# Moving the loading and squaring of x to GpSimd, and the scaling of the memory keys, in the opening of a one-core transformer trunk

## The chip, the cores and the metric

The kernel runs on one core of a Trainium2 chip. Its time is the device time of one execution in microseconds; the time of a kernel is the median of several runs. Three runs of the kernel before gave 2388.71 us as their median, from 2387.78 to 2390.03 us. The execution that the profiler recorded took 2389.53 us by itself, of which the span from the first to the last instruction is 2387.8 us; 1.7 us lie around the span.

The engines are named as the profile names them: PE is TensorE's matrix multiply, PEld its weight load, DVE is VectorE, ACT is ScalarE, POOL is GpSimd, SP is SyncE, which here only issues transfers.

## The reference

The computation is one decoder layer on a sequence of 2048 rows of width 1024, with 256 memory rows, all in float32:

```python
mem_n = rmsnorm(mem, mem_norm_g)
h = rmsnorm(x, mix_norm_g)                       # retention and pooling heads
x = x + concat([y_ret, y_pool]) @ w_out
k, v = split(mem_n @ wkv)                        # cross-attention
s = (rmsnorm(x, xa_norm_g) @ wq) . k             # per head
x = x + softmax(s) . v @ wo
x = x + conv_glu_ffn(rmsnorm(x, ffn_norm_g))
return rmsnorm(x, final_norm_g)
```

What matters here is `mem_n`, `k`, `v`, and the sum of squares of each row of `x` that the first `rmsnorm(x, ...)` needs.

## The kernel before

Every float32 product is made of three matmuls. `split` writes the upper half of a tile (rounded to the matmul's type) with ACT and the lower half (the tile less its upper half) with DVE; `passes` (lines 273 to 279) multiplies upper by upper, upper by lower and lower by upper into one PSUM bank. In the profile the three matmuls have lines 276, 277 and 278; ACT's upper halves have line 264 (267 where a gain is multiplied in), and all of DVE's two-input operations have the helper's line 248, or 256 for the form with a scalar.

The kernel opens with `folded_weights`, a generator that prepares weights in which the memory is folded in. Its steps are named in one table by a letter and a number:

- K0 to K7 project the normalised memory to keys. Each takes one 128x1024 tile of `wkv` and 24 matmuls of 256 columns; two steps share a PSUM bank, so four banks hold the keys.
- V0 to V7 do the same for the values. After each second one its bank is split into `vp4`.
- M0 to M3 fold the keys of one head into the score weights: two row tiles of `wqT` (through `row_pair`) and 48 matmuls of 256 columns, evacuated by ACT (line 564).
- O0 to O3 fold the values into the output weights (evacuated at line 583), W0 to W3 the pooling weights (line 611). Their matmuls have 512 columns.

The keys' banks wait for the memory's norm: after K7, `spread` brings the norm as a row to all partitions through two matmuls (line 382) and ACT (line 387), `scaled_keys` multiplies the four banks by it on DVE, and `parted` splits each into `kp4`, from which the score folds read.

The raw tiles come through SP's queue into nine places of 128x1024 (`raws`: three in `R`, two in `S`, four in `Z`), taken in a ring; a transfer into a place waits until the lower half of the tile that lay there is written. The pairs of halves go into five places (`wides`: in `Q`, the two `E`, and two in `G`), also in a ring: the new pair waits until the matmuls that read the old one are done.

Beside the steps, `load_x_wide` loads the eight 128x1024 tiles of `x`, each behind one of the steps 5, 7, 8, 9, 11, 13, 16 and 18 (counted along the table from 0): a transfer on SP's queue (line 652) into one of the nine places, the split into `X`, a square on ACT (line 654) and an addition on DVE to the first tile. Behind step 21 `rows_norm` takes the row norms from the sum through eight small matmuls (line 357).

The tile framework orders each engine's instructions at build time by its own estimate; what is marked by `keep_in_program_order` keeps its place in the order of the marked ones, and `issue_after` puts an instruction behind another one. At run time each engine takes its instructions strictly in that order. GpSimd issues transfers of its own queue only later (lines 1051 and 1054, behind small copies of `halo` at lines 1070 and 1071 that pace them) and computes nothing else in the opening.

## Time and profile before

| | |
|---|---|
| median of three runs | 2388.71 us |
| the profiled execution | 2389.53 us |
| its span | 2387.8 us |
| PE busy | 2368.7 us, 11136 matmuls |
| DVE busy | 1796.6 us |
| ACT busy | 1385.8 us |
| POOL busy | 337.9 us |
| granted TensorE clock, mean over the span | 0.997 |

The busy time of PE is the sum of its matmuls' spans, overlaps taken out; what is missing to the span is time in which PE had nothing to run. A view of waits says for each engine how long it sat idle and which instruction ended that; the timeline lists instructions with their start and duration and gives the idle time ahead of one in brackets, with its releaser.

### The profile page before, as it was taken

Reading aid. Unit: us, or ns where it says so; the run is one execution under the profiler, and the core shown is the slowest. Engines: PE = TensorE matmul, PEld = TensorE weight load, DVE = VectorE, ACT = ScalarE, POOL = GpSimd, SP = SyncE. Lnnn points to the kernel's source line nnn. Section 1 sums busy time; section 2 is a strip of 40 time slices with the busy share of each in tenths; the row PEclk is TensorE's granted clock in tenths of the full one; section 3 lists DMA queues with packets and bytes.
Section 4 is the critical chain, followed back from the end, with each engine's and each line's share of the span. In section 5 each row is a group of like instructions: output and inputs, shape, how many; then the busy total and the mean of one; then the engine's idle time right before and its main releaser. Section 6 shows DMA issues by size and latency. Waiting matters only on the chain.

```text
span 2387.8 us, 33436 instructions
## 1 busy us (share of the span) xinstructions
PE 2368.7 (99%) x11136; PEld 1980.8 (83%) x11136; DVE 1796.6 (75%) x2977; ACT 1385.8 (58%) x2507; POOL 337.9 (14%) x524
## 2 busy tenths in 40 slices
PE   8999999999999999999999999999999999999998
PEld 8888888888888888888888888888888888888886
DVE  8687876885767677866788776977677698877876
ACT  7845554663545545545655555855555577676663
POOL 0056554453041000000000010110000000000000
PEclk9999999999999999999999999999999999999999
DMA  8999999999594235486577564765455489768951
GB/s 308 343 285 294 280 264 285 284 308 310 164 260 123 79 119 159 151 281 228 170 238 251 179 199 135 243 207 176 150 177 188 136 261 316 234 183 284 343 174 73
DMA packets 269453, 527.78 MB, mean 221 GB/s; under 512 B 30048, under 2 KB 50912, under 8 KB 269280
## 3 DMA queue, kind: packets, MB, share of 16 engines
q1 hardware_dynamic: 212176, 402.83, 51.5%
q0 software_dynamic: 40960, 94.40, 16.5%
q10 hardware_dynamic: 16144, 28.43, 3.2%
q8 instruction: 87, 1.43, 0.2%
q14 instruction: 86, 0.70, 0.1%
HBM read 423.30 MB, written 196.61 MB: 260 GB/s over the span
## 4 chain that ended last, share of the span: by engine, by line
PE 97%; DMA 1%; DVE 1%; ACT 0%; issue 0%; SPq 0%; DVEq 0%; ACTq 0%
PE mm L276 30%; PE mm L278 30%; PE mm L277 30%; PE aux L276 1%; PE aux L278 1%; PE aux L277 1%; PE aux L800 1%; PE aux L774 1%; PE aux L785 1%; PE aux L947 1%; PE aux L802 1%; PE aux L357 0%; DMA S<-w_v 0%; DVE Z L248 0%; DMA Xd<-E 0%; PE aux L776 0%
## 5 line engine op out<-in xcount | busy, mean ns | idle before, releaser
L276 PE MATMUL mm<-G,Q 128*128 128x512 f32 (+1 forms) x1445 | 558.4, 388 | 4.3 <-DVE G L248 2.6
L277 PE MATMUL mm<-G,Q 128*128 128x512 f32 (+1 forms) x1445 | 558.7, 387 | 0.2 <-DVE G L256 0.2
L278 PE MATMUL mm<-G,Q 128*128 128x512 f32 (+1 forms) x1445 | 555.8, 387 | 0.2 <-DVE Q L248 0.2
L277 PE MATMUL mm<-G,E 128*128 128x512 f32 (+1 forms) x1072 | 409.4, 382 | 0.0
L276 PE MATMUL mm<-G,E 128*128 128x512 f32 (+1 forms) x1072 | 408.3, 382 | 0.3 <-DVE Z L248 0.3
L278 PE MATMUL mm<-G,E 128*128 128x512 f32 (+1 forms) x1072 | 408.0, 382 | 0.2 <-DVE E L248 0.2
L276 PEld LDWEIGHTS mm<-G,Q 128*128 128x128 f32 x1445 | 271.4, 188 | 60.2 <-issue 2.7
L277 PEld LDWEIGHTS mm<-G,Q 128*128 128x128 f32 x1445 | 271.5, 188 | 54.4 <-DVE G L248 0.4
L278 PEld LDWEIGHTS mm<-G,Q 128*128 128x128 f32 x1445 | 271.5, 188 | 54.4 <-DVE Q L248 0.4
L256 DVE SCALAR_TENSOR_TENSOR Z<-Z,vecs,Z 128x1024 f32<-128x1024 f32 x176 | 224.6, 1280 | 50.6 <-ACT Z L1219 47.0
L248 DVE TENSOR_TENSOR Z<-Z,mm 128x512 f32<-128x512 f32 (+1 forms) x290 | 193.5, 672 | 90.8 <-PE mm L278 88.8
L278 PEld LDWEIGHTS mm<-G,E 128*128 128x128 f32 x1072 | 201.5, 188 | 39.7 <-DVE E L248 0.6
L276 PEld LDWEIGHTS mm<-G,E 128*128 128x128 f32 x1072 | 201.4, 188 | 39.7 <-DVE Z L248 0.8
L277 PEld LDWEIGHTS mm<-G,E 128*128 128x128 f32 x1072 | 201.5, 188 | 38.9
L248 DVE TENSOR_TENSOR Q<-R,Q 128x512 fp32r<-128x512 f32 (+2 forms) x205 | 139.9, 683 | 84.3 <-ACT Q L1156 48.0
L248 DVE TENSOR_TENSOR T<-T 128x512 f32<-128x512 f32 (+4 forms) x196 | 133.9, 689 | 27.2 <-ACT T L424 13.3
L1156 ACT ACTIVATE Q<-R 128x512 fp32r<-128x512 f32 (+1 forms) x123 | 75.7, 617 | 133.0 <-PE mm L277 126.3
L1156 ACT ACTIVATE E<-R 128x512 fp32r<-128x512 f32 (+1 forms) x163 | 100.3, 615 | 71.0 <-PE mm L277 56.7
L1219 ACT ACTIVATE Z<-Z,vecs 128x1024 f32<-128x1024 f32 x88 | 109.1, 1241 | 32.3 <-DVE Z L248 31.3
L1103 ACT ACTIVATE G<-T 128x512 fp32r<-128x512 f32 x180 | 108.3, 623 | 32.4 <-DMA T<-Gd 22.4
L1156 ACT ACTIVATE Q<-S 128x512 fp32r<-128x512 f32 (+1 forms) x81 | 49.9, 616 | 98.6 <-PE mm L277 95.7
L248 DVE TENSOR_TENSOR Q<-S,Q 128x512 fp32r<-128x512 f32 (+1 forms) x112 | 75.9, 678 | 38.8 <-ACT Q L1156 30.1
(425 smaller groups left out, 4430.8 us busy)
## 6 DMA issues: line engine op xcount, KB each, us to landing
T<-Gd SPq DMA_DIRECT2D x168, 256.0 KB, 4.3
Ud<-w_up POOLq DMA_DIRECT2D x132, 256.0 KB, 9.7
Gd<-Z SPq DMA_DIRECT2D x110, 256.0 KB, 2.6
R<-Ud SPq DMA_DIRECT2D x104, 256.0 KB, 2.7
R<-w_up SPq DMA_DIRECT2D x82, 256.0 KB, 2.9
S<-Ud SPq DMA_DIRECT2D x72, 256.0 KB, 2.8
Gd<-T SPq DMA_DIRECT2D x56, 256.0 KB, 3.3
T<-Xd SPq DMA_DIRECT2D x53, 256.0 KB, 4.1
```

Source lines behind the costliest of these rows:

```text
L248: return eng.tensor_tensor(out=out, in0=a, in1=b, op=op)
L256: return dve.scalar_tensor_tensor(out=out, in0=a, scalar=s, in1=b, op0=op0, op1=op1)
L276: pe.matmul(ps, lh, rh, start=start, stop=False, skip_group_check=more)
L277: pe.matmul(ps, lh, rl, start=False, stop=False, skip_group_check=more)
L278: latest[0] = pe.matmul(ps, ll, rh, start=False, stop=stop, skip_group_check=more)
L774: pe.matmul(col(sc, c), self.ch(k, c), self.ch(q, c), start=True, stop=True)
L785: pe.matmul(col(kv, c), col(self.kn.f, c), self.ch(v, c, h * T), start=True, stop=True)
L800: pe.matmul(col(y, c), col(self.pr.f, c), self.ch(v, c, h * T), start=True, stop=self.cur[c] is None)
L802: pe.matmul(col(y, c), self.ch(q, c), self.cur[c], start=False, stop=True)
L1103: one = act.activation(hi, x, AF.Copy, scale=-1.0 if i == 2 else 1.0)
L1156: act.activation(p2[:, 0, :w], self.raw[i].f[:, :w], AF.Copy)
L1219: act.activation(self.c[g].f, a[:, 2:], AF.Identity, bias=cb[:, f : f + 1], scale=cw[2][:, f : f + 1])
```

## The change

It has two parts.

The tiles of x go another way. Each comes through GpSimd's own queue into a double place of the small temporaries `T`; the first four transfers are paced by a copy on ACT and one on GpSimd (`halo`, columns 41 and 42), the other four follow when a place is free. GpSimd squares each tile in place and adds it to the first. The tiles are fetched behind the steps 8 to 11 and split behind the steps 11, 12, 13, 15, 17, 18, 19 and 20; the row norms follow behind step 22 in place of 21. The nine raw places hold weights alone.

The keys are scaled later. At the end of K7 the tiles of V0 and V1 and both row tiles of M0 are loaded and split ahead of the norm, and each of the four banks is scaled, and its halves written, behind the lower half of M0's second row tile. The multiplication, the halves of the keys, the pairs of V2 and M1 and M0's row pairs are marked to keep their program order. The pooling factors' tile is loaded behind step 5.

```diff
@@ wide_pair, row_pair @@
-        def wide_pair(raw, parts=1):
+        def wide_pair(raw, parts=1, kept=False):
...
-                split(raw[:, i * w : (i + 1) * w], *(r[:, i * w : (i + 1) * w] for r in u))
+                split(raw[:, i * w : (i + 1) * w], *(r[:, i * w : (i + 1) * w] for r in u), kept=kept)
@@ project @@
-            u = u0 if n == 0 else wide_pair(second, 2) if n == 1 else wide_pair(load_tile(wkv[n]))
+            u = u0 if n == 0 else wide_pair(second, 2) if n == 1 else ready.pop(0) if n in (KT, KT + 1) else wide_pair(load_tile(wkv[n]), kept="both" if n == KT + 2 else False)
@@ scaled_keys @@
-            tt(dve, ps3, ps3, both, ALU.mult)
-            parted(kp4, n, ps)
+            tc.keep_in_program_order(tt(dve, ps3, ps3, both, ALU.mult))
+            parted(kp4, n, ps, "both")
@@ keys @@
             if n == KT - 1:
+                for v in (KT, KT + 1):
+                    ready.append(wide_pair(load_tile(wkv[v])))
+                ready.extend(row_pair(wqT[dt * P : (dt + 1) * P, :], "both") for dt in range(2))
+                rows = lowest[0].ins
                 spread(rn, [rm.f[:, :NMEM]], late=True, behind=latest[0].ins)
                 for pair in done:
-                    scaled_keys(*pair)
+                    with tc.issue_after(rows):
+                        scaled_keys(*pair)
@@ score_weights @@
-            dp = [row_pair(wqT[(2 * h + dt) * P : (2 * h + dt + 1) * P, :]) for dt in range(2)]
+            dp = [ready.pop(0) if h == 0 else row_pair(wqT[(2 * h + dt) * P : (2 * h + dt + 1) * P, :], "both" if h == 1 else False) for dt in range(2)]
@@ x @@
-    def load_x_wide(k, total):
-
-        r = total if k == 0 else raws.take()
-        f = r.f
-        tc.keep_in_program_order(sp.dma_start(f, xT[k * P : (k + 1) * P, :T]))
+    def fetch_x_wide(k, gate):
+
+        mark = nullcontext()
+        if gate:
+            here, there = halo[:, 41], halo[:, 42]
+            tc.keep_in_program_order(act.activation(here, phalo[:, 0, :2], AF.Copy))
+            mark = tc.issue_after(pool.tensor_copy(there, here).ins)
+        r = TT.take(2)
+        with mark:
+            tc.keep_in_program_order(pool.dma_start(r.f[:, :T], xT[k * P : (k + 1) * P, :T]))
+        return r
+
+    def load_x_wide(k, r, total):
+
+        f = r.f[:, :T]
         split(f, X[:, 2 * k], X[:, 2 * k + 1], mixg[:, k : k + 1], kept="both")
-        tc.keep_in_program_order(act.activation(f, f, AF.Square))
+        tc.keep_in_program_order(tt(pool, f, f, f, ALU.mult))
         if k:
-            tc.keep_in_program_order(tt(dve, total.f, total.f, f, ALU.add))
+            tc.keep_in_program_order(tt(pool, total.f[:, :T], total.f[:, :T], f, ALU.add))
             r.free()
@@ the steps @@
-    wv, total, x_at = [], raws.take(), (5, 7, 8, 9, 11, 13, 16, 18)
+    wv, x_raws, x_from, x_at = [], [], (8, 9, 10, 11), (11, 12, 13, 15, 17, 18, 19, 20)
...
-        if n == 21:
+        if n == 22:
```

How the instructions move is seen in three places. In the rows below, `Q_79`, `E0_73`, `E1_74` and `G_72` on the left of the arrow are halves of tiles (`G_72` also the halves of keys, values and x), `R_78`, `S4_80`, `S5_81`, `Z2_75` on the right are raw places, `mm...` are PSUM banks, `Z3_76` is the staging of folded weights, `T_77` the temporaries, and the brackets name the semaphores waited for.

The first place is ACT around the first score fold M0. Before, from the upper half of V2's tile (`E1_74`) to the evacuation of M0's first bank (`mm19_492`):

```order
L264 ACTIVATE E1_74<-S5_81 128x1024 [waits DMAHW2_49,Activation_49]
L654 ACTIVATE R_78<-R_78 128x1024 [waits DVE_49]
L264 ACTIVATE G_72<-mm7_146 128x2x256 [waits DVE_49]
L264 ACTIVATE G_72<-mm8_203 128x2x256 [waits DVE_49]
L264 ACTIVATE G_72<-mm13_281 128x2x256 [waits DVE_49]
L264 ACTIVATE G_72<-mm14_340 128x2x256 [waits DVE_49]
L267 ACTIVATE G_72<-Z2_75,vecs_82 128x1024 [waits DMAHW3_49]
L264 ACTIVATE G_72<-mm18_422 128x2x256 [waits PE_49]
L267 ACTIVATE G_72<-Z2_75,vecs_82 128x1024 [waits DMAHW5_49]
L264 ACTIVATE G_72<-R_78 128x1024 [waits DMAHW5_49]
L564 ACTIVATE Z3_76<-mm19_492 128x512 [waits PE_49]
```

In the changed kernel, from the evacuation of M0's third bank (`mm21_509`) on; `Q_79` is V3's tile, `E0_73` a row tile of M2, `E1_74` V2's tile, the first `G_72<-T_77` the first tile of x, and the two rows behind it are M1's row tiles (they differ only in their waits):

```order
L570 ACTIVATE Z3_76<-mm21_509 128x512 [waits PE_49]
L264 ACTIVATE Q_79<-Z2_75 128x1024 [waits DMAHW6_49,PE_49]
L264 ACTIVATE E0_73<-R_78 128x1024 [waits DMAHW7_49,PE_49]
L570 ACTIVATE Z3_76<-mm22_523 128x512 [waits PE_49]
L572 DMA Md_102<-Z3_76 128x2x512 [waits Activation_49]
L665 ACTIVATE halo_96<-phalo_97 128x2 [waits Pool_49]
L264 ACTIVATE E1_74<-Z2_75 128x1024 [waits DMAHW3_49]
L665 ACTIVATE halo_96<-phalo_97 128x2 [waits Pool_49]
L267 ACTIVATE G_72<-T_77,vecs_82 128x1024 [waits DMASW0_49]
L264 ACTIVATE G_72<-Z2_75 128x1024 [waits DMAHW4_49]
L264 ACTIVATE G_72<-Z2_75 128x1024
```

V2's upper half stood ahead of all of M0's evacuations and of the keys' halves; now it stands behind M0's last evacuation and behind two upper halves into `Q` and `E0`, which wait for PE because M0's matmuls read those two places. M1's row tiles stand behind the first tile of x.

The second place is DVE around the scaling of the keys. Before:

```order
L248 TENSOR_TENSOR mm7_146<-mm7_146,T_77 128x512 [waits Activation_49]
L248 TENSOR_TENSOR mm8_203<-mm8_203,T_77 128x512
L248 TENSOR_TENSOR mm13_281<-mm13_281,T_77 128x512
L248 TENSOR_TENSOR mm14_340<-mm14_340,T_77 128x512
L248 TENSOR_TENSOR E0_73<-S4_80,E0_73 128x1024 [waits DMAHW1_49,Activation_49]
L248 TENSOR_TENSOR E1_74<-S5_81,E1_74 128x1024 [waits DMAHW2_49,Activation_49]
L248 TENSOR_TENSOR G_72<-mm7_146,G_72 128x2x256 [waits Activation_49]
```

And in the changed kernel:

```order
L248 TENSOR_TENSOR Q_79<-R_78,Q_79 128x1024 [waits DMAHW0_49,PE_49,Activation_49]
L248 TENSOR_TENSOR E0_73<-R_78,E0_73 128x1024 [waits DMAHW2_49,PE_49,Activation_49]
L248 TENSOR_TENSOR mm7_146<-mm7_146,T_77 128x512
L248 TENSOR_TENSOR G_72<-mm18_423,G_72 128x2x256 [waits Activation_49]
L248 TENSOR_TENSOR G_72<-mm7_146,G_72 128x2x256 [waits Activation_49]
L248 TENSOR_TENSOR mm8_203<-mm8_203,T_77 128x512
L248 TENSOR_TENSOR G_72<-mm8_203,G_72 128x2x256 [waits Activation_49]
```

The four multiplications stood together ahead of M0's second row tile and V2's tile; now M0's two row tiles stand first, and each multiplication is followed by the lower halves of its keys. The lower half of the first two value steps (`mm18_423`) has come between the first multiplication and its keys' lower half.

The third place is ACT at the last tile of x. Before, it stands (from `S4_80`) among the evacuations of O0 and O1 (`mm32_748` is the bank of V4 and V5):

```order
L264 ACTIVATE G_72<-mm32_748 128x2x256 [waits PE_49]
L267 ACTIVATE G_72<-S4_80,vecs_82 128x1024
L264 ACTIVATE E1_74<-R_78 128x1024 [waits DMAHW6_49,DVE_49]
L264 ACTIVATE Q_79<-Z2_75 128x1024 [waits DMAHW2_49,DVE_49]
L583 ACTIVATE Z3_76<-mm41_926,rnm_145 128x4x128 [waits PE_49]
```

In the changed kernel it stands (from `T_77`) behind the bank of V6 and V7 (`mm45_967`) and the first evacuation of W0 (`mm55_1093`):

```order
L264 ACTIVATE G_72<-mm45_967 128x2x256 [waits PE_49]
L621 ACTIVATE Z3_76<-mm55_1093 128x4x128 [waits DMAHW0_49,PE_49]
L267 ACTIVATE G_72<-T_77,vecs_82 128x1024 [waits DMASW7_49]
L621 ACTIVATE Z3_76<-mm56_1098 128x4x128 [waits DMAHW1_49,PE_49]
L264 ACTIVATE Q_79<-R_78 128x1024 [waits DVE_49]
```

The last tile of x has moved behind W0's first matmuls, and the row sums' small matmuls, on PE 39 matmuls of 512 columns behind that first evacuation's bank, wait for GpSimd's last addition.

## The prediction

> **What bounds the kernel now.** I read the page first, then PE's waits in the opening, then the timelines of PE, ACT and DVE around each of those waits, because the change touches nothing behind the opening.

> ```profile
> span 2387.8 us, 33436 instructions
> PE 2368.7 (99%) x11136; PEld 1980.8 (83%) x11136; DVE 1796.6 (75%) x2977; ACT 1385.8 (58%) x2507; POOL 337.9 (14%) x524
> PE 97%; DMA 1%; DVE 1%; ACT 0%; issue 0%; SPq 0%; DVEq 0%; ACTq 0%
> ```

> PE is the bound: 97% of the chain that ended last is matmuls, and 2387.8 less 2368.7 leaves 19.1 us in which PE had nothing to run. The change adds and removes no matmul, so it can only move that idle time, and what the clock loses after it. PE's waits of the first 135 us, in total, times and the longest, hold two that count:

> ```profile
> PE mm L276 <- ACT G L264: 3.0, 2, 2.8
> PE mm L276 <- DVE G L248: 2.6, 1, 2.6
> ```

> PE's timeline (start, duration, and in brackets the idle time ahead with its releaser) shows where they lie and what follows:

> ```profile
> 37.56 0.28 PE L278 MATMUL mm<-G 128*128 128x256 f32 x1
> 40.41 0.35 PE L276 MATMUL mm<-G,Q 128*128 128x256 f32 x1 [2.57 <-DVE G L248]
> ...
> 46.11 0.28 PE L278 MATMUL mm<-G,E 128*128 128x256 f32 x1
> 46.23 0.28 PE L276 MATMUL mm<-G,E 128*128 128x256 f32 x1
> ...
> 56.36 0.39 PE L276 MATMUL mm<-G 128*128 128x256 f32 x1 [2.78 <-ACT G L264]
> ...
> 56.70 0.41 PE L276 MATMUL mm<-G 128*128 128x256 f32 x1
> ...
> 59.91 0.37 PE L277 MATMUL mm<-G 128*128 128x256 f32 x1
> 60.12 0.28 PE L278 MATMUL mm<-G 128*128 128x256 f32 x1
> ```

> The first wait (2.57 us) stands between V1's last matmul and M0's first: the keys' halves are late. M0 then runs into V2 without a gap (46.11 to 46.23, 0.12 us a matmul of 256 columns). The second wait (2.78 us) stands inside M1. Behind it, from 56.70 to 60.12, the matmuls start 0.21 us apart: 16 of them take 3.42 us where 16 times 0.12 is 1.92, so 1.5 us go to a halved clock. The opening thus loses 2.57 + 2.78 + 1.5 = 6.85 us; that is all the change could give back.

> **The change part by part.** The second wait is a transfer's, as the chain of waits shows (start, length):

> ```profile
> 47.34 1.24 DVE R L248
> 48.60 6.63 DMA R<-wqT
> 55.25 1.06 ACT G L264
> ```

> M1's row tile waits for the place in `R` that x's sum of squares held. With x off those places, the changed SP order has M1's tiles right behind V2's, ahead of M0's matmuls: that cause goes, and with it 2.78 us. SP's queue loses eight issues, and nothing else there waited for them. ACT loses eight squares (group of the opening: count, total, mean ns), DVE seven additions of 1.22 us (row 49.62 below), all beside matmuls:

> ```profile
> L654 ACT ACTIVATE Z<-Z 128x1024 f32<-128x1024 f32 x4 | 4.2, 1061 | 0.8 <-DVE G L256 0.8
> ```

> The first wait does not go. These are the durations for it, from the timelines of PE (row sums, then the norm's spread), ACT and DVE, and the landing times of x's transfers on SP's queue:

> ```profile
> 22.97 0.50 PE L357 MATMUL aux<-consts,R 128*128 128x1 f32 x4
> 31.69 0.40 PE L382 MATMUL aux<-Q,ones 128*128 128x256 f32 x2
> 33.58 0.36 ACT L387 ACTIVATE T<-aux 128x256 f32<-128x256 f32 x1
> 36.70 2.03 ACT L264 ACTIVATE G<-mm 128x512 fp32r<-128x512 f32 x4
> 34.91 2.49 DVE L248 TENSOR_TENSOR mm<-mm,T 128x512 f32<-128x512 f32 x4
> 39.58 2.48 DVE L248 TENSOR_TENSOR G<-mm,G 128x512 fp32r<-128x512 f32 x4
> DMA to landing us min/median/max: 5.0/7.9/9.9
> ```

> The spread ends at 32.09, ACT's row at 32.5, M0's two upper halves (0.95 us apart, below) at 34.4, their lower halves at 35.7, the first multiplication (2.49 / 4 = 0.62) at 36.3. That is 1.5 us ahead of V1's end at 37.84, which covers a late row tile: issued behind the row sums at about 23.4, it lands by 23.4 + 9.9 = 33.3 at the worst, 0.8 us late. But in DVE's new order the lower half of V0 and V1 stands between the multiplication and the keys' lower half, and ACT has the same order; that bank is complete only at 37.84. So ACT writes its upper half to 38.5 and the keys' to 39.0 (0.51 each, 0.1 a handover); DVE its lower half to 39.2 and the keys' to 39.8 (0.62 each). M0's first matmul starts at 39.1, its second at 39.95: idle 2.0 us in place of 2.57. Ends: 1.5, and 2.6 if nothing is gained.

> A new wait comes behind M0. For it I need ACT's and DVE's rows of before at the same place, and GpSimd's copy that paces x:

> ```profile
> 46.04 0.58 ACT L564 ACTIVATE Z<-mm 128x512 f32<-128x512 f32 x1
> 46.52 1.05 ACT L264 ACTIVATE Q<-Z 128x1024 fp32r<-128x1024 f32 x1
> 47.46 1.05 ACT L264 ACTIVATE E<-Z 128x1024 fp32r<-128x1024 f32 x1
> 48.41 0.58 ACT L564 ACTIVATE Z<-mm 128x512 f32<-128x512 f32 x1
> 119.33 0.19 ACT L1070 ACTIVATE halo<-consts 128x2 f32<-128x2 f32 x1
> 119.58 0.68 POOL L1071 COPY halo<-halo 128x2 f32<-128x2 f32 x1 [119.13 <-ACT halo L1070]
> 48.49 1.22 DVE L248 TENSOR_TENSOR Q<-Z,Q 128x1024 fp32r<-128x1024 f32 x1
> 49.62 1.22 DVE L248 TENSOR_TENSOR R<-R,Z 128x1024 f32<-128x1024 f32 x1
> ```

> M0's other 47 matmuls run from 39.95 to 45.6. In the new ACT order V2's upper half is queued behind the upper halves into `Q` and `E0`, which wait for M0's last reads, and behind M0's fourth evacuation; the rows of before show those three at 46.52, 47.46 and 48.41, right behind M0's end at 46.23. Nothing is queued there now that PE needs; in the changed kernel PE's next matmul is. ACT gets to it late: the three other banks cost 0.62 + 0.51 + 0.62 and handovers, some 1.9 us each, so the first of them has its upper half at 41.05 and the third at 44.85; the first pacing copy waits for nothing, but the second one, ahead of M0's third evacuation, waits for GpSimd's copy (0.68), until 45.8. Evacuation to 46.3, `Q` to 47.25, `E0` to 48.2, evacuation to 48.7, a pacing copy, V2's upper half to 49.85 and its lower half to 51.1. PE idles from 45.6 to 49.9, runs two matmuls, and idles 0.95 more: 5.25 us. If the pacing cost nothing, `Q` would start at 45.2, 0.4 us ahead of M0's end, and it would be 4.25; with a slower copy, up to 5.9. So the waits are 2.0 + 5.25 = 7.25 in place of 5.35: 1.9 us more.

> The clock's loss I leave at 1.5 us (rows 56.70 to 60.12), at another place: no change. Ends: none, or twice that, since 2.57 us of idle time cost nothing and 2.78 cost 1.5. [...]

> M1's row tiles now stand on ACT and DVE behind the first tile of x, which GpSimd's queue brings. What such a transfer takes is seen later in the trace (timeline of POOL, then the issues, KB each and us to landing):

> ```profile
> 120.19 2.25 POOL L1054 DMA_DIRECT2D Ad<-w_qkgu x4
> 125.72 0.84 POOL L1051 DMA_DIRECT2D Ad<-w_qkgu x1 [2.15 <-DMA Ad<-w_qkgu]
> Ad<-w_qkgu POOLq DMA_DIRECT2D x48, 256.0 KB, 8.4
> ```

> Issued at about 45.7, x lands 5.5 (120.19 to 125.72) to 8.4 us later, at 51.2 to 54.1. Behind it come x's halves and the lower halves of two row tiles, 1.15 + 1.2 + 1.15 + 1.15 = 4.65: 55.9 to 58.8. PE needs the last of these 34 matmuls behind 51.1 (22 of V2, 12 of M1), at 51.1 + 4.1 + 1.5 = 56.7. I take a landing at 52.7: 0.6 us more, ends 0 and 2.1.

> GpSimd's own work is 15 operations of 128x1024 with two inputs, whose kind no row shows. Bounds: the same on DVE takes 1.22 us; of 128x2, GpSimd's copy takes 0.68 us where ACT's takes 0.19, so it is 0.5 longer, or 3.6 times as long: 1.7 to 4.4 us. With two elements a row what differs is a start, not a rate, so I take the lower, 1.7. Its chain starts at x's second tile (squared behind the lower half that ACT and DVE now write last of the first four), about where V4's matmuls begin. From there to the row sums PE has 144 matmuls of 256 columns and 115 of 512. The rate of the wide ones, W's evacuations, and both halves of a tile of x:

> ```profile
> 104.19 0.40 PE L278 MATMUL mm<-Q 128*128 128x512 f32 x1
> 104.42 0.39 PE L277 MATMUL mm<-Q 128*128 128x512 f32 x1
> ...
> 108.17 1.09 ACT L611 ACTIVATE Z<-mm 128x512 f32<-128x512 f32 x2 [0.59 <-PE mm L278]
> 53.77 1.15 ACT L267 ACTIVATE G<-Z,vecs 128x1024 fp32r<-128x1024 f32 x1 [3.21 <-DMA Z<-xT]
> ...
> 43.77 1.27 DVE L256 SCALAR_TENSOR_TENSOR G<-Z,vecs,G 128x1024 fp32r<-128x1024 f32 x1
> ```

> 144 x 0.12 + 115 x 0.23 = 43.7 us for 14 operations and four issues of 0.9: room for 2.85 us an operation. At the end, from W0's first bank to the row sums, PE has 39 x 0.23 = 9.0 us, and against it stand 0.55 (evacuation) + 1.15 and 1.27 (x's halves) + 0.4 (handovers) + two operations: room for 2.8. At 1.7 nothing waits. [...]

> Sum: +1.9 (waits) + 0 (clock) + 0.6 (M1) + 0 (row sums) = +2.5 us. On the profiled execution, 2389.5 us, that gives 2392.0; the median of the runs is 0.8 us below that execution, so I forecast 2391.2. The case's own ends, all of one side at once: -1.1 (4.25, 1.5, no loss of clock, no wait in M1) and +6.8 (5.9, 2.6, twice the loss, 2.1 in M1), so 2387.6 to 2395.5.

> **The rivals.** *GpSimd and DVE hold each other up: slower.* If operations with two inputs in SBUF cannot run on both at once, the time is their sum. Between the lower halves of x's second and last tile stand 12 of GpSimd's operations and, on DVE, 15 such of 128x1024 (1.15 us apart) and 7 of 128x512 (0.62): 20.4 + 21.6 = 42.0 us at 1.7, 55.2 at 2.8 (above which the next rival holds), in the 38.8 us that PE's 34.8 (144 x 0.12 + 76 x 0.23) and the halves around them leave. PE then waits 3.2 to 16.4 us, and 0.5 more for the last two. With the sum: 2395 to 2408, middle 2401.5. It decides from 1.43 us an operation, where the two sums pass 38.8. For it: DVE is busy with two-input work in every stretch here. Against: the trace has no such operation on GpSimd, and its small copies pass beside DVE's. [...]

> *GpSimd alone is too slow: slower.* Over 2.85 us an operation, the row sums wait 14 times the excess: at 3.3, 6.3 us, so 2397.5. For it the bound of 4.4, against it that two elements cannot show a rate.

> *Both waits go: faster.* If V2's halves came in time and the keys' too, 6.85 us less the 0.6 in M1 are won: 2382.5. For it: the first multiplication is done 1.5 us before V1 ends; against it the order of ACT, which is fixed in the program.

> *The change does nothing here.* The stalls only change place and the clock is spared: within the forecast's own range, 2388.7.

> **How the numbers follow.** Forecast 0.47, mutual blocking 0.30, GpSimd too slow 0.14, faster 0.06, no effect 0.03. A measurement of this kernel tells about 0.2% from no change, 4.8 us: bounds 2383.9 and 2393.5. Faster 0.06; slower 0.30 + 0.14 + 0.02 of the forecast's upper end = 0.46; same the remaining 0.48. The range from 2387.6 to 2405 leaves out the faster case and the dearest third of mutual blocking, 0.16 in all; it is wide because blocking has no row.

> **What would show it.** Right: idle of about 2 us ahead of M0 that ends with DVE's lower half; 4 to 6 us behind M0 released by ACT's and DVE's halves into `E`; M1 with little or none; the row sums without a wait for POOL. DVE's 128x1024 rows at 1.22 us between 70 and 110 us, and POOL's at 1.7 to 2.5, speak against blocking; means well above these, with a wait `PE aux <- POOL`, prove it. The forecast is wrong if V2 does not wait, or if PE waits for x's sum.

## The result, and the profile after

The changed kernel takes 2407.56 us (median of 4 runs, 2404.07 to 2412.53) against 2388.65 us before on the same chip: a ratio of 1.008, 95% interval 1.0062 to 1.0099, or 19 us more. The forecast was 2391.2, the range reached to 2405. The profiled execution is the longest of the four, 2412.53 us. Its page, span and engines:

```profile
span 2410.8 us, 33457 instructions
PE 2379.3 (99%) x11136; PEld 1987.9 (82%) x11136; DVE 1810.6 (75%) x2970; ACT 1380.8 (57%) x2503; POOL 395.6 (16%) x551
```

The span is 23.0 us longer. PE runs the same 11136 matmuls, but is busy 10.6 us longer (2379.3 against 2368.7) and idle 12.4 us longer (31.5 against 19.1). The two need different explanations. First the idle time: PE's waits from 30 to 180 us of the span (total, times, longest), which held 5.8 us before and hold 15.7 now.

```profile
PE mm L277 <- ACT E L264: 4.3, 1, 4.3
PE mm L278 <- DVE G L248: 4.0, 2, 3.8
PE mm L278 <- DVE Q L248: 3.0, 1, 3.0
PE aux L358 <- POOL T L248: 2.4, 1, 2.4
PE mm L277 <- DVE G L248: 1.5, 1, 1.5
PE mm L279 <- DVE E L248: 0.5, 1, 0.5
```

The 1.5 is the first wait, ahead of M0; the 4.3 and 0.5 stand behind M0, for V2's halves; M1 has no wait any more. These are as forecast. The 3.0 and 3.8, for lower halves that VectorE writes late, and the 2.4 at the row sums, for GpSimd's last addition, are not. GpSimd's timeline, and VectorE's at the same times (start, duration; a row with x2 gives the sum of two):

```profile
79.94 5.26 POOL L248 TENSOR_TENSOR T<-T 128x1024 f32<-128x1024 f32 x2
86.10 5.29 POOL L248 TENSOR_TENSOR T<-T 128x1024 f32<-128x1024 f32 x2
...
118.85 8.43 POOL L248 TENSOR_TENSOR T<-T 128x1024 f32<-128x1024 f32 x2 [5.90 <-DVE G L256]
```

```profile
79.85 3.09 DVE L248 TENSOR_TENSOR G<-R,G 128x1024 fp32r<-128x1024 f32 x1 [5.04 <-ACT Z L570]
82.87 3.42 DVE L248 TENSOR_TENSOR Q<-Z,Q 128x1024 fp32r<-128x1024 f32 x1
86.21 6.26 DVE L248 TENSOR_TENSOR E<-S,E 128x1024 fp32r<-128x1024 f32 x2
...
118.69 1.21 DVE L248 TENSOR_TENSOR Q<-R,Q 128x1024 fp32r<-128x1024 f32 x1
119.83 1.21 DVE L248 TENSOR_TENSOR G<-S,G 128x1024 fp32r<-128x1024 f32 x1
120.97 1.28 DVE L248 TENSOR_TENSOR E<-Z,E 128x512 fp32r<-128x512 f32 x2
122.39 2.69 DVE L248 TENSOR_TENSOR G<-R,G 128x1024 fp32r<-128x1024 f32 x1
```

VectorE's operation beside one of GpSimd's takes 3.09, 3.42, 3.13 us in place of 1.2, and it ends some 1.1 us behind GpSimd's: the pairs of GpSimd's operations end at 85.20 and 91.39, the operations of VectorE beside them at 86.29 and 92.47. In these rows, then, it stands still until GpSimd's is over and then does its own work. Where VectorE has one operation right behind another (from 118.69), it is GpSimd that waits: 8.43 us for two, where the pairs at 79.94 and 86.10 took 5.3. How full that makes VectorE is seen from the busy time of PE, PEld, DVE, ACT and POOL between 80 and 120 us, before and then after (an operation that stands still counts as busy):

```profile
80.00:120.00 40.00, 39.58 (x215) 33.46 (x214) 27.77 (x45) 32.48 (x50) 0.42 (x1) 1.00 0.99 340
```

```profile
80.00:120.00 40.00, 33.17 (x166) 27.52 (x166) 40.00 (x23) 29.20 (x41) 29.76 (x14) 0.91 0.84 267
```

Before, PE was the full one there (39.58 of 40) and VectorE did 45 instructions in 27.77 us; now VectorE shows no free time at all and has got through 23 of its rows.

The busy time: PE's clock. The column behind POOL's is the granted clock. These windows are 3.41 us long:

```profile
46.64:50.05 3.41, 0.00 (x0) 0.00 (x0) 2.36 (x2) 2.96 (x5) 0.90 (x3) 1.00 0.90 295
50.05:53.47 3.42, 2.81 (x11) 2.52 (x12) 3.29 (x3) 3.12 (x5) 2.40 (x3) 0.50 0.81 255
53.47:56.88 3.41, 3.41 (x18) 3.41 (x17) 3.10 (x2) 1.59 (x2) 2.02 (x1) 0.50 1.04 421
...
104.70:108.10 3.40, 0.76 (x5) 0.33 (x3) 3.40 (x3) 2.03 (x3) 1.58 (x2) 1.00 1.08 396
108.10:111.50 3.40, 2.93 (x6) 1.82 (x6) 3.40 (x3) 2.78 (x5) 3.32 (x2) 0.50 1.00 300
111.50:114.90 3.40, 0.00 (x0) 0.00 (x0) 3.40 (x2) 1.81 (x3) 1.45 (x1) 1.00 0.38 119
114.90:118.30 3.40, 3.07 (x7) 2.48 (x8) 3.40 (x6) 1.56 (x3) 0.00 (x0) 0.50 0.16 16
```

In these rows each window in which PE had little to do (0.00, 0.76 and 0.00 us busy) is followed by one at half clock, though PE is busy for 2.81 to 3.07 us by then; behind the wait for V2 it is two. There is a fourth stretch, 128.56 to 135.38, behind the row sums, and a fifth far behind the opening, 609.83 to 613.24. Half clock in a busy window of 3.41 us costs, by my estimate, half of it, 1.7 us (the matmuls of 512 columns start 0.42 us apart from 610.37 on, 0.23 from 602.87 on). Before, there was one such window up to the last 10 us of the span. Taken over slices of 0.2 us, half clock costs 9.5 us of busy time in the opening and 1.7 at 610, against 1.7 before: 9.5 of PE's 10.6 us. Most of the rest is at the very end, where both kernels fall to half clock: there it costs 1.5 us after (2398.42 to 2401.83) and 0.5 before (from 2377.76). The waits sum up to 9.9 in the opening and 2.3 more between 400 and 660 us: 12.2 of the 12.4.

### The profile page after: what moved, and what is told of

It is laid out like the page before. It is cut to its first block, busy times and chain, and to the rows that moved or that the text cites. A ratio compares the mean times of both kernels' runs of the same rounds, so it can differ in the third digit from the quotient of the medians.

```text
span 2410.8 us, 33457 instructions
## 1 busy us (share of the span) xinstructions
PE 2379.3 (99%) x11136; PEld 1987.9 (82%) x11136; DVE 1810.6 (75%) x2970; ACT 1380.8 (57%) x2503; POOL 395.6 (16%) x551
## 3 DMA queue, kind: packets, MB, share of 16 engines
q8 instruction: 87, 1.43, 0.2%
## 4 chain that ended last, share of the span: by engine, by line
PE 93%; DMA 1%; DVE 1%; POOL 0%; ACT 0%; issue 0%; SPq 0%; DVEq 0%; ACTq 0%
PE mm L277 29%; PE mm L279 29%; PE mm L278 29%; PE aux L277 1%; PE aux L279 1%; PE aux L278 1%; PE aux L822 1%; PE aux L796 1%; PE aux L807 1%; PE aux L969 1%; PE aux L824 1%; PE aux L358 1%; DMA S<-w_v 0%; DVE Z L248 0%; DMA Xd<-E 0%; POOL T L248 0%
## 5 line engine op out<-in xcount | busy, mean ns | idle before, releaser
L278 PE MATMUL mm<-G,Q 128*128 128x512 f32 (+1 forms) x1445 | 560.0, 388 | 4.1 <-DVE G L248 4.0
L277 PE MATMUL mm<-G,Q 128*128 128x512 f32 (+1 forms) x1445 | 559.3, 388 | 3.2 <-DVE G L248 1.5
L277 PE MATMUL mm<-G,E 128*128 128x512 f32 (+1 forms) x1072 | 409.6, 383 | 4.6 <-ACT E L264 4.3
L278 PE MATMUL mm<-G,E 128*128 128x512 f32 (+1 forms) x1072 | 410.5, 383 | 0.0
L278 PEld LDWEIGHTS mm<-G,Q 128*128 128x128 f32 x1445 | 272.1, 188 | 59.1 <-DVE G L248 4.9
L277 PEld LDWEIGHTS mm<-G,Q 128*128 128x128 f32 x1445 | 272.0, 188 | 59.0 <-ACT G L264 1.7
L256 DVE SCALAR_TENSOR_TENSOR Z<-Z,vecs,Z 128x1024 f32<-128x1024 f32 x176 | 224.7, 1280 | 50.1 <-ACT Z L1241 45.6
L248 DVE TENSOR_TENSOR Z<-Z,mm 128x512 f32<-128x512 f32 (+1 forms) x290 | 193.6, 672 | 90.9 <-PE mm L279 88.4
L277 PEld LDWEIGHTS mm<-G,E 128*128 128x128 f32 x1072 | 202.5, 189 | 44.2 <-ACT E L264 4.5
L278 PEld LDWEIGHTS mm<-G,E 128*128 128x128 f32 x1072 | 202.6, 189 | 39.0
L248 DVE TENSOR_TENSOR Q<-R,Q 128x512 fp32r<-128x512 f32 (+2 forms) x209 | 143.9, 689 | 89.2 <-ACT Q L1178 48.9
L248 DVE TENSOR_TENSOR T<-T 128x512 f32<-128x512 f32 (+4 forms) x196 | 134.0, 689 | 27.6 <-ACT T L425 13.5
L1241 ACT ACTIVATE Z<-Z,vecs 128x1024 f32<-128x1024 f32 x88 | 109.2, 1242 | 31.0 <-DVE Z L248 30.1
L1178 ACT ACTIVATE Q<-S 128x512 fp32r<-128x512 f32 (+1 forms) x81 | 49.9, 616 | 98.9 <-PE mm L278 96.3
L248 DVE TENSOR_TENSOR E<-aux,E 128x512 fp32r<-128x512 f32 (+1 forms) x136 | 89.2, 658 | 20.7 <-ACT E L1178 15.6
## 6 DMA issues: line engine op xcount, KB each, us to landing
T<-Gd SPq DMA_DIRECT2D x168, 256.0 KB, 4.4
Ud<-w_up POOLq DMA_DIRECT2D x132, 256.0 KB, 9.6
Gd<-Z SPq DMA_DIRECT2D x110, 256.0 KB, 2.7
R<-Ud SPq DMA_DIRECT2D x104, 256.0 KB, 2.7
R<-w_up SPq DMA_DIRECT2D x82, 256.0 KB, 2.9
S<-Ud SPq DMA_DIRECT2D x72, 256.0 KB, 2.8
Gd<-T SPq DMA_DIRECT2D x56, 256.0 KB, 3.3
T<-Xd SPq DMA_DIRECT2D x53, 256.0 KB, 4.1
```

Source lines behind the costliest of these rows:

```text
L248: return eng.tensor_tensor(out=out, in0=a, in1=b, op=op)
L256: return dve.scalar_tensor_tensor(out=out, in0=a, scalar=s, in1=b, op0=op0, op1=op1)
L277: pe.matmul(ps, lh, rh, start=start, stop=False, skip_group_check=more)
L278: pe.matmul(ps, lh, rl, start=False, stop=False, skip_group_check=more)
L1178: act.activation(p2[:, 0, :w], self.raw[i].f[:, :w], AF.Copy)
L1241: act.activation(self.c[g].f, a[:, 2:], AF.Identity, bias=cb[:, f : f + 1], scale=cw[2][:, f : f + 1])
```

## The experiments

Two theories stood at the start. **Blocking**: GpSimd's squares and additions and VectorE's operations exclude each other, which makes halves and sums late. **Elsewhere**: the transfers by GpSimd's queue (A), the new order of keys and row tiles (B), or GpSimd's own length (C) cost it.

### The parts one by one

*Squares and sums off GpSimd*, all else as in the changed kernel:

```
-        tc.keep_in_program_order(tt(pool, f, f, f, ALU.mult))
+        tc.keep_in_program_order(act.activation(f, f, AF.Square))
-            tc.keep_in_program_order(tt(pool, total.f[:, :T], total.f[:, :T], f, ALU.add))
+            tc.keep_in_program_order(tt(dve, total.f[:, :T], total.f[:, :T], f, ALU.add))
```

> x still comes through GpSimd's queue and the keys are scaled as in the changed kernel, but ScalarE squares x and VectorE adds (15 operations off GpSimd). Theory (GpSimd's two-input operations and VectorE's hold each other up): VectorE's 128x1024 halves are back at 1.2 us, the waits of 3.8 and 3.0 us on VectorE and the 2.4 us on GpSimd go, only the 4.3 us behind M0 and 1.5 ahead of it stay; 2391, between 2389 and 2394. Rival A (the transfers of GpSimd's queue and their descriptors slow VectorE): its rows stay at 2.7 us and more, 2403 to 2408. Rival B (the new order of keys and row tiles costs it): 2403 to 2408 with VectorE's rows at 1.2 us.

Measured: 2400.68 against 2391.51 us, ratio 1.0036 (1.0023 to 1.0049). VectorE's groups from 60 to 128 us (count, total, mean ns), and PE's waits:

```profile
L256 DVE SCALAR_TENSOR_TENSOR G<-T,vecs,G 128x1024 fp32r<-128x1024 f32 x7 | 8.8, 1279 | 2.2 <-ACT G L267 2.2
L248 DVE TENSOR_TENSOR G<-R,G 128x1024 fp32r<-128x1024 f32 x4 | 4.9, 1222 | 3.7 <-ACT Z L570 3.1 <-ACT G L264 0.6
```

```profile
PE mm L277 <- ACT E L264: 4.3, 1, 4.3
PE aux L358 <- DVE T L248: 2.2, 1, 2.2
```

All of VectorE's rows of 128x1024 are back at 1.22 to 1.28 us, with x's transfers still on GpSimd's queue: A is out as the cause of the long rows. The waits of 3.0 and 3.8 are gone. But the ratio is above what was expected: the row sums still wait, now for VectorE (they stand earlier in PE's order in this kernel, ahead of W's evacuations), and two stretches of 6.83 us at half clock stay, which cost 5.65 us.

*Only the squares back on ScalarE*: the first pair of lines of that diff alone.

> Only the eight squares go back to ScalarE, the seven additions stay on GpSimd. Theory (mutual blocking): 7 operations of some 2.8 us block in place of 15, the time they take from VectorE is halved and more, and since part of it fell into VectorE's free time most of the loss goes: 2391 to 2398. Rival C (nothing is blocked, GpSimd's chain of 15 is simply too long for the row sums): 2391 to 2393 with VectorE's halves at 1.2 us throughout, the seven additions fitting easily. Rival A or B: 2403 to 2408.

Measured: ratio 1.0042 (1.0027 to 1.0057). The seven additions take 2.4 us each, the last 3.4; VectorE's group `G<-R,G` has a mean of 1473 ns, in the changed kernel 2607. In VectorE's rows that is between the two kernels, as blocking has it; in time it cannot be told from 1.0036. C is out: seven additions in 40 us leave GpSimd idle for more than half of them.

*Only the key part*, and *only the x part*, the rest as before:

> Only the key part of the change: early row tiles and V0 and V1, keys scaled behind the first fold's rows; x as before, through SyncE's queue into the old places, squared on ScalarE and added on VectorE. Theory (blocking): the key part alone costs no more than the order's stalls, 2389 to 2394. Rival B: most of the 19 us is here, 2400 to 2408.

> Only the x part: x in pairs of temporaries by GpSimd's queue, squared and added on GpSimd; keys, V0, V1 and the row tiles as before. Theory (blocking): the loss is here, less the stall behind M0: 2398 to 2406, with VectorE's halves at 2.7 us and more and a wait for GpSimd's sum. Rival B: 2387 to 2391.

Measured: keys alone 1.0065 (1.005 to 1.008), 2408.0 us, where 2389 to 2394 was expected: a miss, and the time is the one that rival B gave. x alone 1.0059 (1.0042 to 1.0076), 2406.6 us, 0.6 above the range expected. The two alone are 15.5 and 14 us, more than the 19 of both together, so the parts don't simply add up. In keys alone V2 is late again (5.2 and 1.9 us), ScalarE having halves and squares of x between M0's last evacuations and V2's half; that is read from its timeline, not tested.

*The x part with its arithmetic off GpSimd*: the first diff on top of x alone.

> x through GpSimd's queue into pairs of temporaries, squared on ScalarE and added on VectorE; keys, V0, V1 and the row tiles as in the kernel before. Theory (blocking by GpSimd's arithmetic, and a price of 1.7 or 3.4 us of clock behind each stall of over 2 us): against x alone with its arithmetic on GpSimd (ratio 1.0059) all waits on VectorE of 3 us and more go, VectorE's rows are at 1.2 us, the stall for the row tile inside M1 is gone too: ratio 0.998 to 1.002. Rival A (x's transfers by GpSimd's queue, or their later landing, cost the time): ratio 1.003 to 1.006.

Measured: ratio 1.0012 (1.0003 to 1.0021). With x through GpSimd's queue there are now four kernels, keys old or new, arithmetic on GpSimd or not:

| ratio to before | arithmetic on ScalarE and VectorE | on GpSimd | GpSimd's arithmetic |
|---|---|---|---|
| keys as before | 1.0012 | 1.0059 | +0.0047, 11 us |
| keys changed | 1.0036 | 1.0080 | +0.0044, 10.5 us |
| the keys' part | +0.0024, 5.7 us | +0.0021, 5.0 us | |

With x in its new places the parts add up: some 11 us for GpSimd's arithmetic, some 5 for the keys, 3 for x in its new places by the other queue. (With x in its old places the keys' part alone cost 15.5 us, as above. The four were timed on more than one chip, each against before; a difference of two carries some 0.002 either way.)

### Does it take two operands?

In place of the products and sums copies, which read one:

```
-        tc.keep_in_program_order(tt(pool, f, f, f, ALU.mult))
+        tc.keep_in_program_order(pool.tensor_copy(f, f) if k else act.activation(f, f, AF.Square))
-            tc.keep_in_program_order(tt(pool, total.f[:, :T], total.f[:, :T], f, ALU.add))
+            tc.keep_in_program_order(pool.tensor_copy(total.f[:, :T], total.f[:, :T]))
```

> Fourteen of GpSimd's fifteen operations are replaced by a copy of the same 128x1024, which reads one operand (the first square goes to ScalarE; the other squares and the sum are left out). Theory (a pair of two-input operations blocks each other): VectorE's 128x1024 halves return to 1.2 us between 60 and 128 us, the waits of 3.8 and 3.0 us go, ratio 1.003 to 1.005 as with squares and sums off GpSimd. Rival (any read of SBUF by GpSimd blocks VectorE for its length): VectorE's halves stay at 2 us and more, ratio 1.005 to 1.009.

Measured: 1.0118 (1.0095 to 1.0141). The time says nothing here, since the row sums have another place in PE's order in this kernel: they run at 135.6 us. Behind the opening PE waits 8.55 us at 175.24 for an upper half; why that one is late was not followed up. The rows do say something. GpSimd, then VectorE:

```profile
80.30 1.05 POOL L678 COPY T<-T 128x1024 f32<-128x1024 f32 x1
...
81.81 1.05 POOL L676 COPY T<-T 128x1024 f32<-128x1024 f32 x1
82.79 1.05 POOL L678 COPY T<-T 128x1024 f32<-128x1024 f32 x1
```

```profile
80.70 4.22 DVE L248 TENSOR_TENSOR G<-R,G 128x1024 fp32r<-128x1024 f32 x1 [3.73 <-ACT Z L570]
```

VectorE's operation, issued at 80.70, ends at 84.92, 1.08 us behind the last copy (83.84): it stood still for three copies, two of which were issued after it. So here a copy that reads one operand blocked as well, 4.22 us in place of 1.2; that rival was right. A copy is over in 1.05 us, so most of VectorE's rows meet none: 3 of its 26 of 128x1024 between 60 and 128 us take over 1.4 us, and the means stay below the rival's 2 us but for `G<-R,G`.

*GpSimd's operations cut in two*: each `tt(pool, ...)` in a loop over the two halves of 512 columns.

> The changed kernel with each of GpSimd's 15 operations of 128x1024 cut into two of 128x512. Theory (GpSimd and VectorE exclude each other by whole instructions): the same total is excluded, VectorE's waits are no longer 2.6 us but up to 1.4 at a time, so its 128x1024 halves take up to 2.6 us and not 3.4; ratio 1.005 to 1.008. Rival (they share a bandwidth, in proportion, not by instructions): no difference to the changed kernel in VectorE's rows, 1.008.

Measured: 1.0066 (1.0044 to 1.0088), whose interval holds the changed kernel's 1.008. The rows went against the expectation: VectorE's `G<-R,G` has a mean of 2864 ns (2607 in the changed kernel) and `G<-T,vecs,G` 2083 (1423), and its longest operation, at 80.67, takes 5.88 us where at most 2.6 was expected. More of VectorE's operations meet one of GpSimd's (12 of 25 of 128x1024 take over 1.4 us, 8 of 25 in the changed kernel); nothing was won. The rival of a shared bandwidth, by which the rows would not change, does not fit them either.

### The stall behind M0 and the clock

*V2's tile early*, loaded and split ahead of the scaled keys, with GpSimd's arithmetic as changed and with it on ScalarE and VectorE:

```
                 rows = lowest[0].ins
+                ready.append(wide_pair(load_tile(wkv[KT + 2]), kept="both"))
```

> The changed kernel, but V2's tile is loaded and split ahead of the scaled keys like V0's and V1's. Theory (each stall of PE costs its own length and then the clock, halved for whole stretches of 3.4 us behind it; the order behind M0 makes one stall, GpSimd's arithmetic against VectorE the others): the 4.3 us behind M0 and the 6.8 us at half clock go, about 7 us less than the changed kernel's ratio of 1.008, so 1.005. Rival (the clock dips belong to the load of the engines, not to stalls): only the 4.3 us go, ratio 1.006, and half speed stays between 50 and 57 us.

> The same, and x squared on ScalarE and added on VectorE, so that GpSimd only issues x's transfers. Theory: of the 10 us of the kernel with squares and sums off GpSimd, the 4.3 us wait and its 2.2 us of clock go; what stays is the wait for the row sums with its half clock, 5.6 us, and the gain of M1's wait: ratio 0.999 to 1.002. Rival (clock by load): ratio 1.002 to 1.004.

Measured: 1.008 (1.0065 to 1.0095) and 1.0051 (1.0034 to 1.0067); neither is better than the kernel without this edit. In the first the wait for V2 and the half clock behind it are gone, as the theory had it (full clock up to 106.7 us), and the time is lost elsewhere: at 199.68 PE waits 3.83 us for VectorE, which has waited 3.59 us for the transfer of `rope_d` (tables of sines that the kernel computes and stores), and half clock stands from 198.90 to 205.72. In the changed kernel no wait between 180 and 390 us is over 0.5 us. In the second the wait for V2 has gone too, and PE waits in M1 instead:

```profile
58.84 0.58 PE L277 MATMUL mm<-G 128*128 128x256 f32 x1 [6.90 <-ACT G L264]
```

```profile
55.35 1.06 ACT L264 ACTIVATE G<-Z 128x1024 fp32r<-128x1024 f32 x1 [2.44 <-DMA Z<-wo]
```

M1's late halves stand on ScalarE behind a tile of `wo` that waits for its transfer. (The profiled execution of this second kernel, 2394.71 us, is the shortest of its four; the others took 2399.96 to 2405.44 us, and what they lost more is not in the trace.) *V2's matmuls ahead of M0's* as well, arithmetic off GpSimd, `(V, 2), (M, 0)` for `(M, 0), (V, 2)` (this edit takes the prepared pairs in another order, so V2 and M0 multiply exchanged tiles; sizes and counts are the same):

> Squares and sums off GpSimd, V2's halves early, and V2's 24 matmuls put ahead of M0's, between V1 and M0. Theory: V2 covers the wait for the keys' halves (1.5 us) and needs nothing that waits for M0, so both stalls and their clock go; the row sums' wait (2.2 us, and up to 3.4 us of clock) stays: ratio 0.999 to 1.002. Rival (the halves of M1's row tiles and V3 take V2's place as what is late, because ScalarE's and VectorE's order behind M0 is the same): ratio 1.003 to 1.005, with a wait of over 3 us in M1 or V3.

Measured: 1.0067 (1.005 to 1.0084), with 8.9 us of waiting in M1. The rival was right, and more than it said: in both kernels the tile that comes next behind M0 is late.

*The stall filled with work*: 34 matmuls without use in front of V2's.

> The changed kernel with 34 extra matmuls of 256 columns, 4.1 us at full clock, between M0's last matmul and V2's first: PE works where it had waited for V2's halves. Theory (a stall of over 3 us is followed by half clock): the wait at 50 us shrinks to under 0.7 us, V2 starts at the same time as before, and the half clock from 50.0 to 57.0 us goes, 3.1 us less than the changed kernel: ratio 1.0065 to 1.007. Rival (the clock by load): half clock stays or grows, ratio 1.008 or more.

Measured: 1.0076 (1.0061 to 1.0091), but no test: the scheduler spread them into M0, which ended later. Pinned behind M0's last matmul:

```
+                with tc.issue_after(latest[0].ins):
+                    for _ in range(34):
+                        pe.matmul(spare[:, :NMEM], kp4[:, 0, 0, :P], kp4[:, 0, 0], start=True, stop=True)
```

> The changed kernel with 34 extra matmuls of 256 columns (4.1 us at full clock) that now stand on PE behind M0's last and ahead of V2's first. Theory (half clock is caused by PE's idle time): V2 starts within 0.3 us of where it starts in the changed kernel, the wait ahead of it is under 0.8 us, and no half clock stands between 48 and 58 us; 3.1 us less than the changed kernel, ratio 1.0065 to 1.007. Rival (the clock follows the load of the other engines and of the transfers): the half clock between 50 and 57 us stays.

Measured: 1.0092 (1.0074 to 1.011). PE's rows at the stall, the clock there, and three of PE's rows with waits later on:

```profile
45.47 4.24 PE L640 MATMUL aux<-G 128*128 128x256 f32 x34
49.93 0.39 PE L277 MATMUL mm<-G,E 128*128 128x256 f32 x1 [0.22 <-ACT E L264]
```

```profile
50.00:53.40 3.40, 2.64 (x20) 2.44 (x21) 2.51 (x3) 2.56 (x3) 1.62 (x3) 1.00 0.85 292
53.40:56.80 3.40, 3.40 (x30) 3.40 (x29) 3.40 (x2) 2.31 (x3) 2.80 (x1) 1.00 1.03 419
```

```profile
112.73 0.80 PE L278 MATMUL mm<-G,Q 128*128 128x512 f32 x1 [6.25 <-DVE G L248]
180.40 0.50 PE L277 MATMUL mm<-G,S 128*128 128x512 f32 x1 [3.10 <-ACT S L1801]
208.00 0.50 PE L279 MATMUL mm<-G,Q 128*128 128x512 f32 x1 [3.07 <-DVE Q L248]
```

The clock's cause is shown: V2 starts at 49.93 (50.20 in the changed kernel), its wait is 0.22, and the clock stays at 1.00 where it was 0.50, with nothing else changed up to there (further on, the row sums come some 18 matmuls later in PE's order). The expected gain is there at first and then lost. The matmul at 112.73 is the one that starts at 115.23 in the changed kernel: PE came to it 5 us sooner, half of that it waits out for VectorE's halves (6.25 us in place of 3.8), and 2.5 us are left. They go behind the opening, in the waits at 180.40 and 208.00, each with a window of half clock behind it (181.75 to 185.16, 209.05 to 212.47); the changed kernel has none of these. Ahead of the second, VectorE has waited 2.62 us for the transfer of `rope_d`. From 80 to 120 us VectorE and not PE sets the pace in the changed kernel.

### The row sums

*Issued later*, by calling them three steps later; and, since that left them where they were in PE's order, *pinned behind the folding's last matmul*:

```
+            with tc.issue_after(latest[0].ins):
+                rn = rows_norm(x_raws[:1])
```

> Squares and sums off GpSimd, and the sixteen small matmuls of the row sums issued three steps of the folding later (behind the value weights), where x's last tile has long been added. Theory: the wait of 2.2 us and the 3.4 us of half clock behind it go, 5.6 us less than with squares and sums off GpSimd alone (ratio 1.0036): 1.001 to 1.002. Rival (the half clock there belongs to the small matmuls or to the load, not to the wait): 1.0025 to 1.0036.

> Squares and sums off GpSimd, and the row sums' small matmuls pinned behind the folding's last matmul, 48 instructions later on PE than in the same kernel without this. Theory: PE does not wait for VectorE's last addition (2.2 us) and the 6.8 us at half clock behind it (3.4 us) go: ratio 1.001 to 1.002 against 1.0036. Rival (half clock there belongs to the sixteen small matmuls): the wait goes and the half clock moves with them, 1.0025 to 1.003.

Measured: 1.0039 (1.0024 to 1.0054), no test of the theory; and 1.0049 (1.0031 to 1.0067), with no wait at the row sums. Against 1.0036 nothing is gained. PE waits 2.59 us at 108.66 for ScalarE's upper half into `Q`, and 3.41 us at half clock follow from 109.2 on all the same. My price for that wait falls: it only came first in a row of late things.

## Why the prediction was wrong

**The step that failed** is the one on GpSimd's own work: "At 1.7 nothing waits." The price of an operation was near enough. In x alone there is one, from 51.57 on, with nothing on VectorE between 51.5 and 53.8 (GpSimd's timeline):

```profile
51.57 1.89 POOL L248 TENSOR_TENSOR T<-T 128x1024 f32<-128x1024 f32 x1 [0.77 <-DVE G L256]
```

That is 1.89 us for a product, and 1.7 was the estimate; an addition took 2.4. That 1.7 came so near is luck, as will be seen. Also the working of the rival *GpSimd and DVE hold each other up* was right: 12 operations of GpSimd and 42 us in all for 38.8 us of room. What failed was the choice between the two, 0.47 against 0.30, on the ground that GpSimd's small copies pass beside VectorE's operations and no row of the trace before shows the pair. Its rows do show it. GpSimd's copies and VectorE's operations in the kernel before, 153.99 with VectorE idle:

```profile
119.46 0.75 DVE L256 SCALAR_TENSOR_TENSOR G<-R,vecs,G 128x512 fp32r<-128x512 f32 x1
153.99 0.20 POOL L1071 COPY halo<-halo 128x2 f32<-128x2 f32 x1
184.93 5.29 POOL L1071 COPY halo<-halo 128x2 f32<-128x2 f32 x1
189.49 0.68 DVE L248 TENSOR_TENSOR Q<-S,Q 128x512 fp32r<-128x512 f32 x1
```

Alone the copy takes 0.20 us. The copy at 119.58 that the prediction read as 0.68 us of work ends at 120.26, where VectorE's operation of 119.46 ends (120.21); the one at 184.93 ends at 190.22, with the last (190.17) of nine operations that VectorE ran back to back. They stood still behind VectorE. So the 0.5 us that the prediction added as a start was waiting time.

That rival stood 10.3 us over the forecast in its middle; the two pairs of the table give 10.5 and 11. Its waits came out: at the measured 1.89 and 2.4 us its sum has 8.5 us of waiting, and measured are 6.8 for VectorE's halves and 2.4 for GpSimd's sum. That the time agrees so well is partly luck: between the profiled executions of the changed kernel and of the one with squares and sums off GpSimd lie 12.7 us, of which 4.8 are PE's busy time, longer by the clock, and the rival's sum has nothing for the clock. The lines that the prediction named as its proof are there: VectorE's rows well above 1.22, and `PE aux <- POOL`. That the two engines exclude each other is in the rows: 4.22 us for a 1.2 us operation beside copies, 8.43 for two of GpSimd's beside a full VectorE. The order of issue alone doesn't say which of them waits: GpSimd's operation of 118.85 let VectorE's of 119.83 and 120.97 pass, and two copies passed VectorE's operation of 80.70; in both places the engine that issued back to back kept the other out. With the copies' rows of before, mutual blocking should have had the larger chance, since at my own price of 1.7 us the two engines' work, 42.0 us, did not fit into the 38.8.

**The clock's term** was mis-sized: 1.5 us, at most twice that, measured 9.5 in the opening of the profiled run (and 5.65 without GpSimd's arithmetic). I took one stall for the whole; the new stalls brought 3.41 to 6.83 us at half clock each. In time it is worth less than in busy time: filling the stall behind M0 kept the clock there and saved nothing in the end.

**The waits by place.** Ahead of M0: 2.0 forecast, 1.65 measured (1.5 and, behind it, 0.15). Behind M0: 5.25 forecast, 4.8 measured (4.3 and 0.5). M1's 2.78 went as forecast, and its new 0.6 didn't come. The row sums: nothing forecast, 2.4 measured. VectorE writes the last tile's half by 118.77, and PE comes to the row sums at 124.9; at 1.89 and 2.4 us GpSimd's last two operations would have been done by 123.1, but beside VectorE they took 8.43. (With VectorE adding the wait is 2.2, but there the row sums stand earlier in PE's order, so that wait says nothing on the room that I had reckoned.) The premise that the change touches nothing behind the opening did not hold: 2.3 us of waits and a window of half clock lie between 400 and 660 us, and their cause stays open.

**The rivals.** GpSimd alone too slow: no, it is 1.89 to 2.4 us. Both waits go: no. No effect: no.

**What isn't settled.** Without GpSimd's arithmetic the forecast of +2.5 us still misses: 1.0036 is 8.6 us. The wait at the row sums (2.2) and what the clock loses more than before (5.65 against 1.7), neither of them in the forecast, come to about the 6 us between. About 5 of the 8.6 belongs to the keys' part by the table; which stall carries it was not isolated, since each edit that removed one brought another. That a cure of the opening is not the answer either, the x part with its arithmetic off GpSimd shows: its waits in the opening are 2.3 us where before has 5.8, and there is no half clock up to 180 us, yet it is 0.12% slower than before. Behind the opening the transfer of `rope_d` comes late, VectorE waits for it, and PE for VectorE:

```profile
182.94 2.50 DVE L248 TENSOR_TENSOR Z<-Z,T 128x512 f32<-128x512 f32 x4 [3.08 <-DMA Z<-rope_d]
186.10 0.50 PE L278 MATMUL mm<-G,Q 128*128 128x512 f32 x1 [2.35 <-DVE Q L248]
```

A window at half clock follows (186.80 to 190.22), and another stands at 592.99. PE is some 4 us ahead of the kernel before at 125 us, while the last load of the tables is issued at 173.19 and before by 169.0: that the opening's gain is lost on this transfer is my reading of it, not a test. V2 early and, in part, the filled stall lost theirs on it too. No version here beats the kernel before.

## What to carry to other kernels

Moving elementwise work from VectorE to GpSimd freed nothing here: beside one of GpSimd's operations VectorE's of 1.2 us took 3.1 to 3.4 us, and GpSimd's arithmetic cost 10.5 to 11 us. Before such a move add up both engines' times as if they were one, and move only what fits into VectorE's free time. Before pricing stalls one by one, look for the engine that is full in that stage and for what comes late behind it: here each stall of PE that was filled or removed came back at the next late tile or transfer, up to 150 us further on.

## What the runs showed of the hardware

Half clock came in steps of 3.413 us in these runs. In the profiled run of the changed kernel it begins or ends at 50.05, 56.88, 108.08, 111.49, 114.90, 118.31, 128.56, 135.38, 609.83 and 613.24; from the first to the ninth are 164 such steps. In the run before, it begins at 56.69 and again at 2377.76, 680 steps on. The length of one wait does not tell which of these windows were followed by half clock. Before, the first wait of 2.57 us lay across a border between two of them (counted back from 56.69), and neither was followed by half clock; in the changed kernel, at 609.83, half clock followed a window with the last 1.2 us of a wait of 1.85 and one of 0.76 us. First the two windows of before, then that of the changed kernel (the first busy column is PE's):

```profile
36.17:39.58 3.41, 1.67 (x14) 1.46 (x13) 3.41 (x6) 3.41 (x6) 0.00 (x0) 1.00 0.03 12
39.58:42.99 3.41, 2.58 (x22) 2.61 (x23) 3.41 (x6) 3.15 (x5) 0.00 (x0) 1.00 0.92 281
```

```profile
606.42:609.83 3.41, 1.47 (x5) 0.94 (x6) 3.28 (x6) 3.09 (x7) 0.00 (x0) 1.00 0.42 152
609.83:613.24 3.41, 3.41 (x10) 2.65 (x9) 3.41 (x6) 1.46 (x3) 0.00 (x0) 0.50 0.31 100
```
